# Final norm fused into one VectorE operation and the last two steps of the down product joined, in a one-core streaming-encoder block

## The chip, the cores and the metric

The kernel runs on one core of one Trainium2 chip. Its metric is the device time of one execution in microseconds (us); given is the median of three runs. The engines are TensorE (PE in the profile; PEld are its weight loads), VectorE (DVE), ScalarE (ACT), GpSimd (POOL) and SyncE (SP), which issues all the DMAs spoken of here.

## The reference

One trunk layer on x of 2048 tokens by 1024 features, in float32: a norm and an input projection, two mixer groups (a gated recurrence and stick-breaking attention), an output projection, then a SwiGLU feed-forward part and the final norm. Only its last lines matter here:

```python
h2 = rms_norm(x, norm_ffn[l])
gu = jnp.einsum('bsd,df->bsf', h2, w_ffn_in[l])
x = x + jnp.einsum('bsf,fd->bsd', jax.nn.silu(gu[..., :D_FF]) * gu[..., D_FF:], w_ffn_out[l])
return rms_norm(x, norm_final)      # x * rsqrt(mean(x * x) + 1e-6) * norm_final
```

## The kernel before, in words

The change lies in the last part, the product with `w_ffn_out` (2816 x 1024), called Down here, and the final norm. Down multiplies by Strassen's scheme: seven products (`DOWN`), each of one 512-wide combination of weight columns with a combination of activations. Its inner dimension comes in six steps (`NCH`): five of two blocks of 128 rows and a last one of one block. "Step (6,3)" is step 3 of product 6, the last product; the names of the profile leave the numbers out, so `blo` of step (6,3) is written `blo6_3` here.

- `operands` (L1116) loads a step's weights (`dr`, two loads and a sum on VectorE, L1135) and activations (`act`) and splits each into a rounded part, a cast on ScalarE (`bhi`, `a0hi`, `a1hi`, L1140), and the remainder, a subtraction (L1141): `blo` on VectorE, `a0lo` and `a1lo` on GpSimd. It is called two steps ahead (`LEAD`); each part has three buffers, so a cast for step c waits until TensorE has finished step c-3.
- `down_step` (L855) runs TensorE over two halves of 1024 tokens, and in a half over four row tiles of 128: per tile and block three matmuls (`mm3`, L149 to L151: `bhi` with `ahi`, `blo` with `ahi`, `bhi` with `alo`). A step of two blocks is 48 matmuls, the last one 24. A product's sums stay in eight banks of PSUM (`pw`); in its last step `use` (L1189) is called after each tile, and `add` (L1145) adds the tile to the residual `x2` (names `x`) on VectorE.
- A half has eight row tiles of output, 0 to 3 lower and 4 to 7 upper, each with two column halves, 0 and 1. Product 6 adds only to column half 0 of the lower tiles; all else is final once product 5 has ended.
- `finish` (L1154) squares and sums a tile's column half on ScalarE (`sqo`) and multiplies it by the final norm's weight on GpSimd (`o<-x,gfin`, L1164). `write` (L1166) computes the root for some tiles on VectorE: a sum (`ssp`, L1169) and 13 more tiny operations (`rsqrt_mean`, L124 to L137, names `ro_`). It then scales each `o` by the root: column half 0 on VectorE (L1181), 1 on ScalarE (L1179); one tile alone is done in a fused operation (L1176). It stores `o` from SP (L1182).

TensorE's instructions run in the order in which they are written. On the other engines a scheduler orders the instructions when the program is built, by its own estimate of when each is ready; each engine and SP then keep that order. `o` has twelve buffers (`OB`).

Of the kernel before, what the change touches and what calls it, by code (L numbers as in the profile page):

```python
# [9 lines left out]
F32 = mybir.dt.float32  # L10
# [3 lines left out]
ALU = mybir.AluOpType  # L14
# [3 lines left out]
P = 128  # L18
# [9 lines left out]
GT = 512  # L28
HT = 1024
NG = S // GT  # L30
TPG = GT // P
NHALF = S // HT
TPH = HT // P
# [34 lines left out]
DOWN = (  # L68
# [7 lines left out]
)  # L76
# [14 lines left out]
def tile_block(ctx: ExitStack, tc: tile.TileContext, x, w_in, w_out, w_gu, w_dn,  # L91
               g_mix, g_ffn, g_y, g_fin, lru_p, w_gate, out):
    nc = tc.nc
# [21 lines left out]
    NCH = -(-NPAIR // CH)  # L115
# [315 lines left out]
    for g in range(NG):  # L431
        starts.append(len(items))
        for h in range(H):
            for jj in range(TPG // 2):
                p = None
# [283 lines left out]
    end = []  # L719
# [132 lines left out]
    ps_u = banks.enter_context(tc.tile_pool(name="ps_u", bufs=2, space=PSUM, side="left"))  # L852
    pss = {}

    def down_step(p, c, bs, aa, use=None):  # L855

        m = len(bs)
        for half in range(NHALF):
            for t in range(TPG):
                if c == 0:  # L860
                    pss[half, t] = ps_u.tile([P, GT], F32, tag="abcd"[t], name=f"pw{half}_{p}_{t}")
                ts = slice(t * P, (t + 1) * P)
                for i, ((bhi, blo), (ahi, alo)) in enumerate(zip(bs, aa[half])):
                    mm3(pss[half, t], ahi[:, ts], alo[:, ts], bhi, blo,
                        c == 0 and i == 0, c == NCH - 1 and i == m - 1)
                if c == NCH - 1:
                    use(half, t, pss[half, t])


# [228 lines left out]
    with tc.manual_schedule(engines={mybir.EngineType.PE}), ExitStack() as dctx:  # L1098
        bp = dctx.enter_context(tc.tile_pool(name="bp", bufs=3, side="right"))
        x2p = dctx.enter_context(tc.tile_pool(name="x2p", bufs=1, side="left"))  # L1100
        op = dctx.enter_context(tc.tile_pool(name="op", bufs=OB, side="left"))
        gfin = x2p.tile([P, D], F32, name="gfin")

        x2s = {}

        def rows(half):
            if half not in x2s:
                x2s[half] = []
                for t in range(TPH):
                    xt = x2p.tile([P, D], F32, tag=f"x2_{half}_{t}", name=f"x2_{half}_{t}")  # L1110
                    gt = half * TPH + t
                    nc.sync.dma_start(out=xt, in_=x2_d[gt // TPG][gt % TPG * P:(gt % TPG + 1) * P, :])
                    x2s[half].append(xt)
            return x2s[half]

        def operands(p, c):  # L1116

            m = min(CH, NPAIR - c * CH)
            nm = f"{p}_{c}"
            ta = DOWN[p][0]  # L1120
            bb = []
            for j, k, _ in ta:
                t = bp.tile([P, m, GT], F32, tag="raw", name=f"dr{nm}_{j}{k}", bufs=4)
                r0 = c * CH * 2 * P
                src = w_dn[r0:r0 + 2 * m * P, k * GT:(k + 1) * GT].rearrange("(m j p) c -> j p m c", j=2, p=P)
                nc.sync.dma_start(out=t, in_=src[j])
                bb.append(t)
            aa = []
            for half in range(NHALF):
                sa = bp.tile([P, m, GT], F32, tag="act", name=f"act{half}_{nm}", bufs=4)  # L1130
                nc.sync.dma_start(out=sa, in_=act_d[half][p][c])
                aa.append(sa)
            sb = bb[0]
            if len(ta) == 2:
                nc.vector.tensor_tensor(out=sb, in0=bb[0], in1=bb[1], op=ALU.add if ta[1][2] > 0 else ALU.subtract)  # L1135
            out = []
            for q, src, eng in (("b", sb, nc.vector), ("a0", aa[0], nc.gpsimd), ("a1", aa[1], nc.gpsimd)):
                hi = bp.tile([P, m, GT], F32R, tag=f"{q}hi", name=f"{q}hi{nm}")
                lo = bp.tile([P, m, GT], F32R, tag=f"{q}lo", name=f"{q}lo{nm}")
                nc.scalar.copy(hi, src)  # L1140
                eng.tensor_tensor(out=lo, in0=src, in1=f32(hi), op=ALU.subtract)  # L1141
                out.append([(hi[:, i], lo[:, i]) for i in range(m)])
            return out

        def add(half, p, t, ps):  # L1145
            x2 = rows(half)
            for i, k, sign in DOWN[p][1]:
                xs = x2[i * TPG + t][:, k * GT:(k + 1) * GT]
                if sign > 0:
                    nc.vector.tensor_tensor(out=xs, in0=ps, in1=xs, op=ALU.add)  # L1150
                else:
                    nc.vector.tensor_tensor(out=xs, in0=xs, in1=ps, op=ALU.subtract)

        def finish(half, t0, n, ss, os, parts):  # L1154

            x2 = rows(half)
            for t in range(t0, t0 + n):
                for c in parts:
                    cs = slice(c * GT, (c + 1) * GT)
                    sq = op.tile([P, GT], F32, tag="sq", name=f"sqo{half}_{t}_{c}", bufs=1)  # L1160
                    nc.scalar.activation(sq, x2[t][:, cs], AF.Square, accum_out=ss[:, t, c:c + 1])  # L1161
                    o = os[t, c] = op.tile([P, GT], F32, tag="o", name=f"o{half}_{t}_{c}")
                    if (half, t, c) != (NHALF - 1, TPG - 1, 0):
                        nc.gpsimd.tensor_tensor(out=o, in0=x2[t][:, cs], in1=gfin[:, cs], op=ALU.mult)  # L1164

        def write(half, t0, n, ss, os):  # L1166
            x2 = rows(half)
            s2 = smp.tile([P, n], F32, tag=f"ssp{n}", name=f"ssp{half}_{t0}")
            nc.vector.tensor_tensor(out=s2, in0=ss[:, t0:t0 + n, 0], in1=ss[:, t0:t0 + n, 1], op=ALU.add)  # L1169
            rs = rsqrt_mean(s2, n, D, f"ro{half}_{t0}")  # L1170
            for t in range(t0, t0 + n):
                for c in range(2):
                    cs = slice(c * GT, (c + 1) * GT)
                    r = rs[:, t - t0:t - t0 + 1]
                    if (half, t, c) == (NHALF - 1, TPG - 1, 0):
                        nc.vector.scalar_tensor_tensor(out=os[t, c], in0=x2[t][:, cs], scalar=r, in1=gfin[:, cs],  # L1176
                                                       op0=ALU.mult, op1=ALU.mult)
                    elif c == 1:
                        nc.scalar.activation(os[t, c], os[t, c], AF.Copy, scale=r)  # L1179
                    else:  # L1180
                        nc.vector.tensor_scalar(out=os[t, c], in0=os[t, c], scalar1=r, scalar2=None, op0=ALU.mult)  # L1181
                    nc.sync.dma_start(out=out[half * HT + t * P:half * HT + (t + 1) * P, cs], in_=os[t, c])  # L1182

        work = [(p, c) for p in range(len(DOWN)) for c in range(NCH)]
        ready = [operands(*w) for w in work[1:1 + LEAD]]
        ss = [smp.tile([P, TPH, 2], F32, tag=f"sso{half}", name=f"sso{half}", bufs=1) for half in range(NHALF)]
        os = [{} for _ in range(NHALF)]

        def use(half, t, ps):  # L1189
            add(half, p, t, ps)  # L1190
            if p == len(DOWN) - 1:
                finish(half, t, 1, ss[half], os[half], (0,))
                if half == 0 and t == TPG - 1:
                    write(half, 0, TPG, ss[half], os[half])
                elif half and t >= TPG - 2:
                    write(half, *((0, TPG - 1) if t == TPG - 2 else (t, 1)), ss[half], os[half])

        for n, (p, c) in enumerate(work[1:]):
            bs, *aa = ready.pop(0)
            if n + 1 + LEAD < len(work):  # L1200
                ready.append(operands(*work[n + 1 + LEAD]))
            if n < NHALF:
                rows(n)
            if n == NHALF:
                nc.sync.dma_start(out=gfin, in_=g_fin.broadcast_to([P, D]))
            down_step(p, c, bs, aa, use)

            if p == len(DOWN) - 1 and c < NHALF:
                for t in range(TPG, TPH):
                    finish(c, t, 1, ss[c], os[c], (0, 1))  # L1210
                    if t % 2:
                        write(c, t - 1, 2, ss[c], os[c])
            if p == len(DOWN) - 1 and NHALF <= c < 2 * NHALF:
                finish(c - NHALF, 0, TPG, ss[c - NHALF], os[c - NHALF], (1,))
    banks.close()


# [51 lines left out]
```

## Time and profile before

| | us |
|---|---|
| median of 3 runs (2645.66 to 2648.19) | 2646.09 |
| profiled execution, its own time | 2647.3 |
| its span in the trace | 2645.6 |
| TensorE busy, 12680 matmuls | 2430.8 |
| VectorE busy | 1842.4 |
| ScalarE busy | 1262.6 |
| GpSimd busy | 1204.0 |

The span is the time from the first to the last instruction in the trace; times below are in us from its start. Busy time is summed over instructions; as they overlap at their ends, a busy engine need not be at its peak. In the view by time a row's two numbers are its start and how long it took, from its dispatch on, so that time in which an operation stood blocked is in it. An arrow in square brackets says how long the engine had been idle before the row and what ended that. The granted clock is a share of full speed: 1.00 is 2.4 GHz, 0.50 is 1.2 GHz.

### The profile page before, as it was taken

What the parts mean: (1) busy time and instruction counts of PE and PEld (TensorE: products, weight loads), DVE (VectorE), ACT (ScalarE), POOL (GpSimd) and SP (SyncE); (2) the same over time, 40 slices, a digit from 0 to 9 for tenths busy, and PEclk for the clock granted to TensorE, in tenths of its full rate; (3) what the DMA queues carried; (4) which work ended last, traced back from release to release, by engine and by line L of the source; (5) the groups of instructions that cost most, each with busy time, mean ns of one, the idle gap of its engine ahead of it and who ended that gap; (6) DMA issues with size and microseconds to landing.
All of it is one profiled execution on the core that took longest, in us unless ns stands there. A gap on an engine that the chain in (4) does not pass through costs nothing. (4 is left out here: it accounts for less than half of the span.)

```text
span 2645.6 us, 36918 instructions
## 1 busy us (share of the span) xinstructions
PE 2430.8 (92%) x12680; PEld 2046.7 (77%) x12680; DVE 1842.4 (70%) x2575; ACT 1262.6 (48%) x2285; POOL 1204.0 (46%) x1420
## 2 busy tenths in 40 slices
PE   7999999999888797897899979989999999999995
PEld 5888788787767697886777758868888887888884
DVE  4566888999999998997655545686655651644465
ACT  5556667576766575664333323343333322322233
POOL 5846433223244121122656654555545544744464
PEclk9999999999999898998999989999999999999997
DMA  7787886664556465654334443353232318745652
GB/s 249 266 288 250 269 267 211 209 210 143 176 179 208 152 223 169 206 188 151 123 121 137 157 167 100 108 177 114 100 103 97 111 69 323 257 153 183 196 172 104
DMA packets 221804, 468.57 MB, mean 177 GB/s; under 512 B 22704, under 2 KB 63664, under 8 KB 221616
## 3 DMA queue, kind: packets, MB, share of 16 engines
q1 hardware_dynamic: 221616, 466.21, 52.8%
q8 instruction: 100, 1.64, 0.3%
q14 instruction: 88, 0.72, 0.1%
HBM read 333.74 MB, written 132.38 MB: 176 GB/s over the span
## 5 line engine op out<-in xcount | busy, mean ns | idle before, releaser
L360 POOL MEMSET u<- 128x1 f32 x320 | 30.9, 98 | 559.2 <-DVE u L372 394.6
L372 DVE TENSOR_TENSOR_SCAN u<-u,u,zero 128x513 f32<-128x513 f32 x192 | 256.2, 1336 | 8.5 <-ACT u L362 8.0
L393 PE MATMUL t<-ident,be 128*128 128x128 f32 x1088 | 179.3, 281 | 59.0 <-DVE al L395 50.0
L378 DVE TENSOR_TENSOR be<-be,u 128x512 f32<-128x512 f32 (+2 forms) x320 | 215.4, 676 | 17.0 <-POOL be L366 1.4
L362 ACT ACTIVATE u<-z 128x512 f32<-128x512 f32 (+2 forms) x320 | 172.4, 539 | 99.1 <-PE z L358 65.2
L149 PE MATMUL pj<-ht_hi,w_hi 128*128 128x512 f32 x512 | 215.8, 421 | 2.3 <-DVE sl L291 1.5
L394 ACT CAST ah<-t 128x512 fp32r<-128x512 f32 (+2 forms) x320 | 168.7, 527 | 86.2 <-PE t L393 82.1
L393 PEld LDWEIGHTS t<-ident,be 128*128 128x128 f32 x1088 | 130.7, 143 | 98.5 <-DVE al L395 64.5
L151 PE MATMUL pj<-ht_hi,w_lo 128*128 128x512 f32 x512 | 202.8, 396 | 0.0
L150 PE MATMUL pj<-ht_lo,w_hi 128*128 128x512 f32 x512 | 201.9, 394 | 0.0
L358 PE MATMUL z<-ks,qd 128*128 128x512 f32 (+2 forms) x640 | 190.9, 380 | 7.1 <-ACT be L363 5.0
L395 DVE TENSOR_TENSOR al<-t,ah 128x512 fp32r<-128x512 f32 (+2 forms) x320 | 191.4, 599 | 7.5 <-ACT ah L394 7.1
L1088 POOL TENSOR_TENSOR e<-c,c 128x512 f32<-128x512 f32 x110 | 158.6, 1449 | 52.0 <-DVE c L1079 37.5
L363 ACT ACTIVATE be<-z 128x512 f32<-128x512 f32 (+2 forms) x320 | 172.5, 539 | 0.2
L408 PE MATMUL y<-ah,vs 128*128 128x256 f32 x576 | 149.9, 290 | 12.3 <-DVE yp L418 12.2
L149 PE MATMUL po<-wo_hi,yhi 128*128 128x256 f32 x512 | 154.9, 303 | 0.0
L372 DVE TENSOR_TENSOR_SCAN u<-u,zero 128x129 f32<-128x129 f32 (+3 forms) x128 | 112.3, 878 | 56.6 <-POOL u L366 55.0
L1141 DVE TENSOR_TENSOR blo<-dr,bhi 128x1024 fp32r<-128x1024 f32 (+1 forms) x41 | 81.8, 1995 | 98.5 <-ACT bhi L1140 98.5
L408 PE MATMUL y<-al,vs 128*128 128x256 f32 x576 | 147.8, 287 | 0.0
L151 PE MATMUL po<-wo_hi,ylo 128*128 128x256 f32 x512 | 145.7, 285 | 0.0
L150 PE MATMUL po<-wo_lo,yhi 128*128 128x256 f32 x512 | 145.6, 284 | 0.0
L1141 POOL TENSOR_TENSOR a0lo<-act,a0hi 128x1024 fp32r<-128x1024 f32 (+1 forms) x41 | 97.8, 2385 | 103.2 <-ACT a0hi L1140 103.2
(284 smaller groups left out, 7624.7 us busy)
## 6 DMA issues: line engine op xcount, KB each, us to landing
r<-in_w_gu SPq DMA_DIRECT2D x88, 512.0 KB, 3.9
act<-act_d SPq DMA_DIRECT2D x68, 512.0 KB, 4.2
dr<-in_w_dn SPq DMA_DIRECT2D x59, 512.0 KB, 4.5
act_d<-e SPq DMA_DIRECT2D x110, 256.0 KB, 2.0
w_hi<-w_d SPq DMA_DIRECT2D x50, 512.0 KB, 4.7
w_lo<-w_d SPq DMA_DIRECT2D x50, 512.0 KB, 5.5
vs<-vs_d SPq DMA_DIRECT2D x80, 256.0 KB, 3.6
ks<-ks_d SPq DMA_DIRECT2D x80, 256.0 KB, 3.6
```

Of the source, the lines that this page charges most:

```text
L149: nc.tensor.matmul(ps, lhsT=w_hi, rhs=m_hi, start=first, stop=False, skip_group_check=more)
L150: nc.tensor.matmul(ps, lhsT=w_hi, rhs=m_lo, start=False, stop=False, skip_group_check=more)
L151: nc.tensor.matmul(ps, lhsT=w_lo, rhs=m_hi, start=False, stop=last, skip_group_check=more)
L358: nc.tensor.matmul(z[:, :nz], lhsT=qd[:, i, qs], rhs=kss[p.c][:, :nz], start=i == 0, stop=i == 1)
L362: nc.scalar.activation(u[:, :n], z[:, :n], AF.Sigmoid, scale=-SCALE)
L363: nc.scalar.activation(be[:, :n], z[:, :n], AF.Sigmoid, scale=SCALE)
L372: nc.vector.tensor_tensor_scan(out=ur, data0=ur, data1=zero.broadcast_to([P, n + 1]), initial=1.0 if p.prev is None else p.prev.u[s][:, 0: ...
L378: nc.vector.tensor_tensor(out=p.be[s][:, :n], in0=p.be[s][:, :n], in1=p.u[s][:, 1:n + 1], op=ALU.mult)
L393: nc.tensor.transpose(tp[:, b, :], p.be[s][:, b * P:(b + 1) * P], ident)
L395: nc.vector.tensor_tensor(out=alo[:, :nb, s, :], in0=tp[:, :nb, :], in1=f32(ahi[:, :nb, s, :]), op=ALU.subtract)
L408: nc.tensor.matmul(y, lhsT=vs[:, b, :], rhs=t[:, b].rearrange("p s q -> p (s q)"), start=first and m == 0, stop=last and m == 1)
L1141: eng.tensor_tensor(out=lo, in0=src, in1=f32(hi), op=ALU.subtract)
```

## The change

Four things. The multiplication by `gfin` and the scaling by the root become one operation on VectorE (`x * r * gfin`) for all column halves but those of column half 1 of the lower tiles, which stay as they were. The upper tiles of a half get one root for four tiles instead of two roots for two, and they and the lower column halves 1 are now treated half by half over the steps (6,0) to (6,3). Half 1's lower tiles get roots for two, one and one tile instead of three and one. And steps (6,4) and (6,5) are run together: for each row tile nine matmuls in a row, then its `use`.

```diff
-    def down_step(p, c, bs, aa, use=None):
+    def down_step(p, c, bs, aa, use=None, end=None):
+        end = c == NCH - 1 if end is None else end
...
-                        c == 0 and i == 0, c == NCH - 1 and i == m - 1)
-                if c == NCH - 1:
+                        c == 0 and i == 0, end and i == m - 1)
+                if end:
                     use(half, t, pss[half, t])
...
-                    o = os[t, c] = op.tile([P, GT], F32, tag="o", name=f"o{half}_{t}_{c}")
-                    if (half, t, c) != (NHALF - 1, TPG - 1, 0):
+                    if t < TPG and c:
+                        o = os[t, c] = op.tile([P, GT], F32, tag="o", name=f"o{half}_{t}_{c}")
                         nc.gpsimd.tensor_tensor(out=o, in0=x2[t][:, cs], in1=gfin[:, cs], op=ALU.mult)
...
-                    if (half, t, c) == (NHALF - 1, TPG - 1, 0):
+                    if (t, c) not in os:
+                        os[t, c] = op.tile([P, GT], F32, tag="o", name=f"o{half}_{t}_{c}")
                         nc.vector.scalar_tensor_tensor(out=os[t, c], in0=x2[t][:, cs], scalar=r, in1=gfin[:, cs],
                                                        op0=ALU.mult, op1=ALU.mult)
-                    elif c == 1:
+                    else:
                         nc.scalar.activation(os[t, c], os[t, c], AF.Copy, scale=r)
-                    else:
-                        nc.vector.tensor_scalar(out=os[t, c], in0=os[t, c], scalar1=r, scalar2=None, op0=ALU.mult)
...
-                elif half and t >= TPG - 2:
-                    write(half, *((0, TPG - 1) if t == TPG - 2 else (t, 1)), ss[half], os[half])
+                elif half and t:
+                    write(half, *((0, 2) if t == 1 else (t, 1)), ss[half], os[half])
...
+            if n == len(work) - 3:
+                held = bs, aa
+                continue
+            if n == len(work) - 2:
+                bs, aa = held[0] + bs, [x + y for x, y in zip(held[1], aa)]
             down_step(p, c, bs, aa, use)
 
-            if p == len(DOWN) - 1 and c < NHALF:
-                for t in range(TPG, TPH):
-                    finish(c, t, 1, ss[c], os[c], (0, 1))
-                    if t % 2:
-                        write(c, t - 1, 2, ss[c], os[c])
-            if p == len(DOWN) - 1 and NHALF <= c < 2 * NHALF:
-                finish(c - NHALF, 0, TPG, ss[c - NHALF], os[c - NHALF], (1,))
+            if p == len(DOWN) - 1 and c < 2 * NHALF:
+                half, late = c // 2, c % 2
+                finish(half, TPG + 2 * late, 2, ss[half], os[half], (0, 1))
+                if late:
+                    write(half, TPG, TPG, ss[half], os[half])
+                    finish(half, 0, TPG, ss[half], os[half], (1,))
```

How the instructions stand on the engines shows three places. In these rows `o0_4_1` is half 0, tile 4, column half 1, `ssp1_4` the sum of half 1 that begins with tile 4, and the last number of a name tells buffers apart.

On VectorE, the operations ahead of `blo6_3`, before (the tiny ones of each root but the first and last left out):

```order
L1169 TENSOR_TENSOR ssp0_4_25527<-sso0_23027 128x2
...
L1181 TENSOR_SCALAR o0_4_0_25513<-o0_4_0_25513,ro0_4_y2_25552 128x512
L1181 TENSOR_SCALAR o0_5_0_25521<-o0_5_0_25521,ro0_4_y2_25552 128x512
...
L1181 TENSOR_SCALAR o0_6_0_25564<-o0_6_0_25564,ro0_6_y2_25603 128x512
L1181 TENSOR_SCALAR o0_7_0_25572<-o0_7_0_25572,ro0_6_y2_25603 128x512
L1169 TENSOR_TENSOR ssp1_4_25698<-sso1_23028 128x2
...
L1181 TENSOR_SCALAR o1_4_0_25684<-o1_4_0_25684,ro1_4_y2_25723 128x512
L1181 TENSOR_SCALAR o1_5_0_25692<-o1_5_0_25692,ro1_4_y2_25723 128x512
L1141 TENSOR_TENSOR blo6_3_25623<-dr6_3_10_25613,bhi6_3_25622 128x1024
```

and now:

```order
L1142 TENSOR_TENSOR blo6_2_25444<-dr6_2_10_25434,bhi6_2_25443 128x1024
L1170 TENSOR_TENSOR ssp0_4_25596<-sso0_23027 128x4
...
L1178 SCALAR_TENSOR_TENSOR o0_4_0_25623<-x2_0_4_23055,ro0_4_y2_25621,gfin_22990 128x512
...
L1178 SCALAR_TENSOR_TENSOR o0_7_1_25644<-x2_0_7_23061,ro0_4_y2_25621,gfin_22990 128x512
L1136 TENSOR_TENSOR dr6_5_10_25740<-dr6_5_10_25740,dr6_5_11_25742 128x512
L1142 TENSOR_TENSOR blo6_3_25529<-dr6_3_10_25519,bhi6_3_25528 128x1024
```

One root of 14 tiny operations and eight fused ones now stand ahead of `blo6_3`, where three roots and six scalings stood. The other root and the other eight fused operations of the upper tiles stand between `blo6_3` and `blo6_4`.

On GpSimd, the instructions around the subtractions for step (6,4), before:

```order
L1141 TENSOR_TENSOR a1lo6_3_25631<-act1_6_3_25619,a1hi6_3_25630 128x1024
L1164 TENSOR_TENSOR o0_0_1_25855<-x2_0_0_23047,gfin_22990 128x512
...
L1164 TENSOR_TENSOR o1_2_1_25948<-x2_1_2_23133,gfin_22990 128x512
L1141 TENSOR_TENSOR a0lo6_4_25798<-act0_6_4_25788,a0hi6_4_25797 128x1024
L1164 TENSOR_TENSOR o1_3_1_25952<-x2_1_3_23135,gfin_22990 128x512
L1141 TENSOR_TENSOR a1lo6_4_25802<-act1_6_4_25790,a1hi6_4_25801 128x1024
L1141 TENSOR_TENSOR a0lo6_5_25883<-act0_6_5_25873,a0hi6_5_25882 128x512
```

and now, with what each waits for (DMAHW is a lane of DMAs, here a store or a load that must have landed):

```order
L1142 TENSOR_TENSOR a1lo6_3_25537<-act1_6_3_25525,a1hi6_3_25536 128x1024 [waits DMAHW3_49,PE_49,Activation_49]
L1142 TENSOR_TENSOR a0lo6_4_25677<-act0_6_4_25667,a0hi6_4_25676 128x1024 [waits DMAHW5_49,PE_49,Activation_49]
L1165 TENSOR_TENSOR o1_0_1_25870<-x2_1_0_23129,gfin_22990 128x512 [waits DMAHW3_49,DMAHW1_49,DVE_49]
L1165 TENSOR_TENSOR o1_1_1_25874<-x2_1_1_23131,gfin_22990 128x512 [waits DMAHW4_49,DMAHW2_49,DVE_49]
L1142 TENSOR_TENSOR a1lo6_4_25681<-act1_6_4_25669,a1hi6_4_25680 128x1024 [waits DMAHW6_49,PE_49,Activation_49]
L1165 TENSOR_TENSOR o1_2_1_25878<-x2_1_2_23133,gfin_22990 128x512 [waits DMAHW5_49,DVE_49]
L1165 TENSOR_TENSOR o1_3_1_25882<-x2_1_3_23135,gfin_22990 128x512 [waits DMAHW6_49,DVE_49]
L1142 TENSOR_TENSOR a0lo6_5_25754<-act0_6_5_25744,a0hi6_5_25753 128x512 [waits DMAHW1_49,PE_49,Activation_49]
```

The four multiplications of half 1 now stand behind `a0lo6_4`, two of them ahead of `a1lo6_4` and all ahead of `a0lo6_5`; `o1_0_1` takes the buffer of half 1's `o1_4_0`, so it waits for a store of half 1's upper tiles.

On TensorE, the first row tile of the end, before (rows that read alike left out):

```order
L149 MATMUL pw0_6_0_25455<-bhi6_4_25793,a0hi6_4_25797 128x512
...
L151 MATMUL pw0_6_0_25455<-bhi6_4_25793,a0lo6_4_25798 128x512
...
L151 MATMUL pw1_6_3_25504<-bhi6_4_25793,a1lo6_4_25802 128x512
L149 MATMUL pw0_6_0_25455<-bhi6_5_25878,a0hi6_5_25882 128x512
L150 MATMUL pw0_6_0_25455<-blo6_5_25879,a0hi6_5_25882 128x512
L151 MATMUL pw0_6_0_25455<-bhi6_5_25878,a0lo6_5_25883 128x512
```

and the first row tile now:

```order
L149 MATMUL pw0_6_0_25455<-bhi6_4_25672,a0hi6_4_25676 128x512
...
L151 MATMUL pw0_6_0_25455<-bhi6_4_25672,a0lo6_4_25677 128x512
L149 MATMUL pw0_6_0_25455<-bhi6_5_25749,a0hi6_5_25753 128x512
L150 MATMUL pw0_6_0_25455<-blo6_5_25750,a0hi6_5_25753 128x512
L151 MATMUL pw0_6_0_25455<-bhi6_5_25749,a0lo6_5_25754 128x512
L149 MATMUL pw0_6_1_25462<-bhi6_4_25672,a0hi6_4_25676 128x512
```

The three matmuls with step (6,5)'s operands follow six of step (6,4) in the same row tile, where they followed all 48.

## Rows read from the trace of the kernel before

**Rows 1.** The page's first line.
```profile
span 2645.6 us, 36918 instructions
```

**Rows 2.** Windows: length, each engine's busy time (instructions), granted clock, DMA share, GB/s.
```profile
2590.00:2600.00 10.00, 9.55 (x30) 7.70 (x31) 8.16 (x15) 4.04 (x11) 7.33 (x5) 0.69 0.42 147
...
2605.00:2610.00 5.00, 2.34 (x5) 1.68 (x6) 3.39 (x2) 4.10 (x10) 3.77 (x3) 0.64 0.00 2
```

**Rows 3.** Waits from 2480 us: who for whom, total us, times, longest.
```profile
PE pw L150 <- DVE blo L1141: 10.9, 2, 8.8
...
PE pw L149 <- ACT bhi L1140: 1.5, 1, 1.5
```

**Rows 4.** TensorE by time: start, duration, engine, line, operation, [idle before <-released by].
```profile
2570.38 0.39 PE L149 MATMUL pw<-bhi,a0hi 128*128 128x512 f32 x1
...
2581.26 0.39 PE L149 MATMUL pw<-bhi,a0hi 128*128 128x512 f32 x1
...
2590.45 0.80 PE L150 MATMUL pw<-blo,a0hi 128*128 128x512 f32 x1 [8.80 <-DVE blo L1141]
...
2603.65 0.39 PE L151 MATMUL pw<-bhi,a1lo 128*128 128x512 f32 x1
...
2605.54 0.50 PE L149 MATMUL pw<-bhi,a0hi 128*128 128x512 f32 x1 [1.50 <-ACT bhi L1140]
...
2608.16 0.79 PE L150 MATMUL pw<-blo,a0hi 128*128 128x512 f32 x1 [2.12 <-DVE blo L1141]
...
2621.77 0.39 PE L151 MATMUL pw<-bhi,a0lo 128*128 128x512 f32 x1
...
2626.53 0.39 PE L151 MATMUL pw<-bhi,a1lo 128*128 128x512 f32 x1
```

**Rows 5.** VectorE by time, same columns.
```profile
2552.32 1.53 DVE L1135 TENSOR_TENSOR dr<-dr,dr 128x1024 f32<-128x1024 f32 x1 [0.80 <-DMA dr<-in_w_dn]
...
2580.26 2.29 DVE L133 TENSOR_TENSOR ro_a<-ro_y 128x2 f32<-128x2 f32 x1
...
2582.58 1.18 DVE L135 TENSOR_TENSOR ro_b<-ro_a,ro_v 128x2 f32<-128x2 f32 x1
...
2589.18 1.22 DVE L1141 TENSOR_TENSOR blo<-dr,bhi 128x1024 fp32r<-128x1024 f32 x1
...
2598.53 0.16 DVE L135 TENSOR_TENSOR ro_b<-ro_a,ro_v 128x2 f32<-128x2 f32 x1
...
2598.72 0.16 DVE L137 SCALAR_TENSOR_TENSOR ro_y<-ro_b,ro_y 128x2 f32<-128x2 f32 x1
...
2600.15 0.88 DVE L1181 TENSOR_SCALAR o<-o,ro_y 128x512 f32<-128x512 f32 x2
```

**Rows 6.** GpSimd by time.
```profile
2580.16 2.37 POOL L1141 TENSOR_TENSOR a1lo<-act,a1hi 128x1024 fp32r<-128x1024 f32 x1
...
2582.49 4.92 POOL L1164 TENSOR_TENSOR o<-x,gfin 128x512 f32<-128x512 f32 x4
```

**Rows 7.** ScalarE by time.
```profile
2600.14 1.34 ACT L1179 ACTIVATE o<-o,ro_y 128x512 f32<-128x512 f32 x2 [6.00 <-issue]
...
2604.45 1.04 ACT L1140 CAST bhi<-dr 128x1024 fp32r<-128x1024 f32 x1
```

**Rows 8.** The end by time, VectorE and ScalarE.
```profile
2622.20 4.09 DVE L1150 TENSOR_TENSOR x<-pw,x 128x512 f32<-128x512 f32 x6 [12.11 <-PE pw L151]
...
2622.98 0.63 ACT L1161 ACTIVATE sqo<-x 128x512 f32<-128x512 f32 x1 [13.81 <-DVE x L1150]
...
2623.52 0.19 ACT L1161 ACTIVATION_READ_ACCUMULATOR sqo<-x 128x1 f32 x1
...
2638.32 0.74 DVE L1176 SCALAR_TENSOR_TENSOR o<-x,ro_y,gfin 128x512 f32<-128x512 f32 x1
```

**Rows 9.** SP's last store; stores from 2630 us: count, size, median us to landing.
```profile
2641.50 0.59 SPq L1182 DMA_DIRECT2D out<-o  x1
...
out<-o SPq DMA_DIRECT2D x16, 256.0 KB, 2.8
```

## The prediction

> **What bounds it now.** I read the page first, then the waits of TensorE in the last 100 us, then one engine after another in order of time. The span is 2645.6 us [rows 1]; everything the diff touches lies after 2541 us, so only this stretch counts. The reader is to see that TensorE loses its granted clock there: mean 0.69 and 0.64 in two windows [rows 2]. It stops for `blo`, 10.9 us in two waits, and for `bhi`, 1.5 us [rows 3]. In time [rows 4]: step (6,2) begins at 2570.38 and (6,3) at 2581.26, so 48 matmuls take 10.88 us, 0.2267 each. The second matmul of (6,3) comes at 2590.45 instead of 2581.49; step (6,4) begins at 2605.54, 1.89 after the matmul before it, and its second matmul waits until 2608.16. From the start of (6,3) to the last matmul, 2626.53, are 119 intervals: 26.98 us at full clock, 45.27 in fact. **18.3 us** are lost: 13.0 in the three late starts (8.96, 1.66, 2.39), 5.3 in matmuls after them at the 1.2 GHz level, before the clock is back at 2.4.
>
> Why are the operands late? `blo6_3` takes only 1.22 us, but starts at 2589.18, and VectorE had no idle time before it [rows 5]: it was busy with other work. Ahead of it on VectorE stand three roots of 14 tiny operations. Such an operation, given a quiet GpSimd, follows the one before at 0.195 us (2598.53 to 2598.72) [rows 5]. But the one at 2582.58 takes 1.18 and the one at 2580.26 takes 2.29 [rows 5], while GpSimd does four multiplications in 4.92 us and, from 2580.16, a 2.37 us subtraction [rows 6]: VectorE gets one in per GpSimd instruction. `bhi6_4` is late in turn: ScalarE stood 6.00 us before a scaling that needs the same slow root, and the cast comes only at 2604.45 [rows 7].
>
> **The change, part by part.** GpSimd loses 23 of 31 multiplications by `gfin`, some 23 x 1.23 = 28 us. ScalarE loses 8 of 16 scalings, those ahead of the casts. VectorE has six roots instead of seven (84 tiny operations, not 98), and 24 fused operations (0.74 us, the only row of its kind, without GpSimd beside it [rows 8]) instead of 15 scalings (two in 0.88 [rows 5]) and one fused: 24 x 0.74 - 15 x 0.44 - 0.74 = 10.4 us more. That extra is hidden only while VectorE has its `blo` ready before TensorE asks, so I walk through it.
>
> *To `blo6_3`.* VectorE starts with the sum `dr6_4`, released by its load at 2552.32 [rows 5]. Then: that sum and `blo6_2`, 2 x 1.22; 14 tiny, 2.73; eight fused, 5.92; sum `dr6_5`, 0.68 (the adds of [rows 8], 4.09 for six); `blo6_3`, 1.22: 13.0 us. GpSimd has three subtractions (2.37) and four multiplications (1.23): 12.0. If none of it overlaps, `blo6_3` ends at 2577.3; TensorE asks at 2581.49. GpSimd idles at the start, since its cast `a0hi6_3` now stands behind two more squares on ScalarE; I credit 2 us of overlap for that and take 2575.4. So the first stall goes, with 4 to 6 us to spare.
>
> *To the joined step.* It starts at 2581.26 + 10.88 = 2592.14 and asks for `blo6_4` at 2592.37, `blo6_5` at 2593.73 and `a0lo6_5` at 2593.95; before, the last two were asked for 48 matmuls, 10.9 us, later. The change adds a wait here: GpSimd's multiplication `o1_0_1` reuses the buffer of `o1_4_0`, so it waits until that has been written out, and `a1lo6_4`, `a0lo6_5` and `a1lo6_5` queue behind it. The second root ends at 2575.4 + 2.73 = 2578.1, the first fused at 2578.9, its write lands 2.8 later [rows 9]: 2581.7, when five fused operations are done. From there I alternate, one by one: 1.23, fused 0.74, 1.23, fused, `a1lo6_4` 2.37, fused, 1.23, `blo6_4` 1.22 (2591.2), 1.23, `blo6_5` 0.68 (2593.1), `a0lo6_5`, taken as another 1.23 (2594.4). The first two are in time by 0.6 to 1.2 us, the last is 0.5 late. I charge **0.5 us** and no loss of clock, which shows only after the stops of 8.96 and of 1.66 with 2.39 [rows 4]. The bounds of the uncovered price: fused operations at the 0.68 of a two-input add and more overlap give 0; no overlap at all is rival 1. The casts `bhi6_4` and `a0hi6_4` have no scaling ahead of them any more and wait only for buffers, free at 2570; all are early. On SP the two loads `act6_5` move ahead of four stores, behind the eight of half 0: issued near 2574, they feed `a0lo6_5` and `a1lo6_5`, which start after 2593. Covered.
>
> *The tail.* Before, 19.07 us lie between the last matmul and the end. Now the last matmul is at 2581.26 + 26.98 + 0.5 = 2608.7. Tile 3 of half 0 is done 36 matmuls into the joined step, its last one at 2600.6, its add 0.43 later (as 2622.20 follows 2621.77 [rows 4, 8]), the square 0.78 after that, its sum 0.73 later still [rows 8]: 2602.5. Root and two adds, 2.73 + 2 x 0.68: 2606.6. Four fused, 2.96: 2609.6. The add of the last tile starts behind them and one more add at 2610.4, its sum of squares is ready at 2611.9, and then come about 15 interleaved tiny operations (1.2), two fused, three tiny, one fused, nine tiny in a chain (1.75), the last fused: 6.4 us, so 2618.3, and the last store at 2618.8. Before, the last store was issued at 2641.50, 4.1 before the end, behind others; alone, it cannot be shorter than about a landing, 2.8 [rows 9]. Of these bounds I take the middle, 3.4: **2622.2**. The tail shrinks from 19.07 to 13.5 us, by 5.6.
>
> **Sum.** 18.3 - 0.5 + 5.6 = 23.4 us off the span of 2645.6, so 2622.2. The profiled execution took 2647.3, 1.7 more than its span, and would take 2623.9; it lies 1.2 above the median of the runs, 2646.09. Forecast for the median: **2622.7 us**, 0.9% less.
>
> The rule that speaks against it: the Trainium skill, "SBUF — State Buffer", section "Who interferes with whom", says that VectorE instructions with two SBUF inputs and GpSimd's reads of SBUF share one read interface, and that whoever comes second stands fully blocked. The rows of the tiny operations agree (1.18 us for 0.16 of work). By it a fused operation, with two inputs from SBUF, is as exposed as what it replaces; rival 1 is what that makes of the time here.
>
> **Rivals.**
> 1. *The exchange stays one for one where it matters.* For: eight fused operations stand directly ahead of `blo6_4`, and six GpSimd instructions fall beside them. With no overlap from 2577.3: VectorE 2.73 + 5.92 + 1.22 + 0.68, GpSimd 5 x 1.23 + 2.37, 19.1 in all: `a0lo6_5` at 2596.4, 2.5 late. Like the stop of 1.66 and 2.39, that may halve the clock, 2.6 us (half of the 5.3). Against the forecast 2.0 + 2.6 more: **2627**. Against: GpSimd stands still until 2581.7.
> 2. *The tiny operations are slow of themselves*, not through GpSimd. Then 14 take 17.1 us: `blo6_3` at 2579.6, still in time, but `blo6_4` at 2579.6 + 17.1 + 5.9 + 1.2 = 2603.8, 11.4 late, with 2.6 of clock. 18.3 - 14.0 + 5.6 = 9.9 off: **2636**. Against: the same operations at 0.195 in a later root.
> 3. *Slower.* TensorE stops inside the joined step for `a0lo6_5`, because GpSimd waits for a store. It decides if the first store of half 1 lands late: every us after 2581.1 costs one. To lose the 23.4 and 5.3 more it must land near 2610, as it would if VectorE's queue before it were delayed by 28 us; GpSimd has 12 us of work there. That gives **2652**. Only an order on the queues that I misread allows it.
> 4. *The change doesn't do what it says*: TensorE is given back its time, but half clock or the stores' rate (eight stores on the queue) sets the end: 2640 to 2646.
>
> **Numbers.** Forecast (2618 to 2625) 0.70; rival 1 0.15; rival 2 0.05; rival 4 0.07, of which 0.05 within the bound below; rival 3 0.03. A measurement here can tell about 0.2%, 5.3 us, from no change. The range runs from no stall and fused operations at the 0.68 of an add (eight on the tail's path, 0.5 us less, and 0.5 of stall), with 3.5 us for the rough parts of the tail, 2618, to rival 1 with 3 us more, 2630. Faster 0.92, same 0.05, slower 0.03.
>
> **What would show it.** Right: tiny operations near 0.2 us from 2571 on; no wait of `pw` for `blo` over 1 us; granted clock 1.00 until the last matmul, near 2608.7; the last fused operation near 2618. Rival 1: a wait for `blo6_4` or `a0lo6_5` of 2 us and a dip of the clock after 2592. Rival 2: tiny operations of 1.2 us beside an idle GpSimd. Rival 3: a wait for `a0lo`, GpSimd idle for a store beyond 2585. The prediction is wrong if step (6,3) still waits, or if the tail takes over 16 us.

## The result and the profile after

| | before | after |
|---|---|---|
| median of 4 runs each, us | 2645.93 | **2611.67** (2608.38 to 2616.12) |
| ratio, 95% interval | | 0.987 (0.9851 to 0.9888) |
| profiled execution's own time | 2647.3 | 2616.12 |
| start of step (6,3) | 2581.26 [rows 4] | 2574.84 |
| start of the last matmul | 2626.53 [rows 4] | 2601.81 |
| span | 2645.6 [rows 1] | 2614.4 |

Faster by 1.3%, 34.3 us between the medians. The forecast was 2622.7, the range 2618 to 2630: the time lies below it. The profiled execution happens to be the slowest of the four, so the spans differ by less, 31.2 us.

The page of after, its first line:

```profile
span 2614.4 us, 36856 instructions
```

TensorE by time (start, duration; no row from 2500 us on shows idle time before it), and two windows over this stretch, to compare with [rows 2]:

```profile
2574.84 0.39 PE L149 MATMUL pw<-bhi,a0hi 128*128 128x512 f32 x1
...
2585.72 0.39 PE L149 MATMUL pw<-bhi,a0hi 128*128 128x512 f32 x1
...
2601.81 0.39 PE L151 MATMUL pw<-bhi,a1lo 128*128 128x512 f32 x1
```

```profile
2570.00:2606.00 36.00, 32.20 (x143) 26.32 (x141) 27.19 (x74) 10.38 (x24) 12.92 (x7) 1.00 0.35 129
2590.00:2600.00 10.00, 10.00 (x46) 8.26 (x44) 6.08 (x21) 3.70 (x11) 0.00 (x0) 1.00 0.01 2
```

From the start of (6,3) to that of the last matmul are 26.97 us, where before took 45.27: the three late starts and the half clock, 18.3 us, are gone to the last tenth, and the granted clock stays at 1.00. VectorE by time shows why:

```profile
2549.15 2.31 DVE L133 TENSOR_TENSOR ro_a<-ro_y 128x4 f32<-128x4 f32 x1
2551.50 1.22 DVE L135 TENSOR_TENSOR ro_b<-ro_a,ro_v 128x4 f32<-128x4 f32 x1
...
2559.48 7.54 DVE L1178 SCALAR_TENSOR_TENSOR o<-x,ro_y,gfin 128x512 f32<-128x512 f32 x8
...
2567.54 1.21 DVE L1142 TENSOR_TENSOR blo<-dr,bhi 128x1024 fp32r<-128x1024 f32 x1
...
2570.65 0.16 DVE L133 TENSOR_TENSOR ro_a<-ro_y 128x4 f32<-128x4 f32 x1
2570.85 0.16 DVE L135 TENSOR_TENSOR ro_b<-ro_a,ro_v 128x4 f32<-128x4 f32 x1
...
2571.24 9.60 DVE L1178 SCALAR_TENSOR_TENSOR o<-x,ro_y,gfin 128x512 f32<-128x512 f32 x8
2580.77 4.00 DVE L1142 TENSOR_TENSOR blo<-dr,bhi 128x1024 fp32r<-128x1024 f32 x2
...
2609.77 0.75 DVE L1178 SCALAR_TENSOR_TENSOR o<-x,ro_y,gfin 128x512 f32<-128x512 f32 x1
```

and GpSimd beside it:

```profile
2549.03 2.42 POOL L1142 TENSOR_TENSOR a0lo<-act,a0hi 128x1024 fp32r<-128x1024 f32 x1 [2.97 <-ACT a0hi L1141]
2551.40 5.08 POOL L1165 TENSOR_TENSOR o<-x,gfin 128x512 f32<-128x512 f32 x4
...
2574.24 3.25 POOL L1165 TENSOR_TENSOR o<-x,gfin 128x512 f32<-128x512 f32 x2 [11.09 <-DMA out<-o]
...
2584.18 1.74 POOL L1142 TENSOR_TENSOR a0lo<-act,a0hi 128x512 fp32r<-128x512 f32 x1
```

While GpSimd works (2549 to 2559) VectorE gets one tiny operation in per GpSimd instruction, 1.22 or 2.31 us, as in [rows 5]. While GpSimd stands 11.09 us for the store of `o1_4_0`, the second root runs at 0.2 us an operation. When GpSimd is back, the eight fused operations take 9.60; the first eight, with one subtraction of GpSimd beside them, took 7.54.

So this stretch gave 24.8 us: from the start of (6,3) to the end are 39.56 us, before 64.34. But (6,3) itself starts 6.42 us earlier, in code that the change does not touch, and that part the prediction did not have. TensorE's matmuls ahead of it stand in the same order in both programs. What differs is where the tiles lie. The small buffers of the roots are allocated early, one set for each number of tiles; the changed kernel has no root for three tiles any more, that set is gone, and all that is allocated behind it on the left of SBUF lies 416 bytes lower. TensorE's operands in the up stage (the product with `w_ffn_in`, 44 rounds of seven products of twelve matmuls, 1250 to 2172 us in the changed kernel), by the built programs, in bytes in a partition:

| | before | after |
|---|---|---|
| weights of products 0 and 6 | 67456 | 67040 |
| tokens of product 0 (as those of products 1 to 4, on the right) | 135136 | 135136 |
| tokens of product 6 (on the left) | 36736 | 36320 |
| tokens less weights modulo 256: product 0, product 6 | 96, 0 | 0, 0 |

In all rounds, products 0 to 4 are 96 bytes apart before and 0 now: 2640 of the stage's 3696 matmuls.

### The profile page after: what moved, and what is told of

The parts are those of the page before. It is cut to its first block, busy times and chain, and to the rows that moved or that the text cites. A ratio compares the mean times of both kernels' runs of the same rounds, so it can differ in the third digit from the quotient of the medians.

```text
span 2614.4 us, 36856 instructions
## 1 busy us (share of the span) xinstructions
PE 2417.2 (92%) x12680; PEld 2046.0 (78%) x12680; DVE 1837.1 (70%) x2569; ACT 1258.0 (48%) x2277; POOL 1174.2 (45%) x1397
## 4 chain that ended last, share of the span: by engine, by line
PE 43%; DVE 3%; DMA 2%; POOL 2%; issue 2%; ACT 1%; SPq 0%; POOLq 0%; DVEq 0%; ACTq 0%
PE pw L151 5%; PE pw L150 5%; PE pw L149 5%; PE psc L149 3%; PE psa L149 3%; PE psc L150 3%; PE psc L151 3%; PE psa L150 3%; PE psa L151 3%; PE psd L149 3%; PE psd L150 3%; PE psd L151 3%; PE psb L149 1%; PE psb L150 1%; PE psb L151 1%
## 5 line engine op out<-in xcount | busy, mean ns | idle before, releaser
L360 POOL MEMSET u<- 128x1 f32 x320 | 31.2, 99 | 558.0 <-DVE u L372 393.4
```

## The experiments

Times are medians, and ratios with their 95% interval are to the kernel before on the same chip (2647.94 for experiments 1, 2, 6 and 7, 2647.83 for 4 and 5, 2647.00 for 8, 2646.68 for 9). The changed kernel's 2611.67 stands beside a before of 2645.93; where a run on another chip is set against it, the difference by the two ratios is given too.

**1. The change at the old addresses.**

```diff
     smp = ctx.enter_context(tc.tile_pool(name="smp", bufs=2))
+    ctx.enter_context(tc.tile_pool(name="padp", bufs=1)).tile([P, 104], F32, name="pad")
```

> The changed kernel with one unused tile of 416 bytes behind the small pool, so that the large tiles lie again at the SBUF addresses that they had before the change (the program is otherwise the same). Theory A (the time won ahead of product 6 comes from the addresses, which the change moved by 416 bytes when the roots for three tiles went): between 1780 and 2200 us about 1780 matmuls, as before, not 1802; product 5's last adds about 6.4 us later than in the changed kernel; time 2611.7 + 6.4 = 2618, up to 2622. Theory B (chance, the traces differ from execution to execution): about 1802 matmuls and 2608 to 2616. Both: the end from product 5's adds on unchanged, no wait of TensorE.

Measured 2622.15 us (0.9902; 0.9887 to 0.9917), 10.5 more than the changed kernel, 8.5 by the ratios. Step (6,3) starts at 2583.00, 8.2 later. In its trace the two products' pace differs. The first matmuls of product 6 (`psb<-b`), of the next product 0 (`psa<-b`) and of product 1 (`psc<-t`):

```profile
1301.94 0.39 PE L150 MATMUL psb<-b,a1h 128*128 128x512 f32 x1
...
1304.66 0.40 PE L150 MATMUL psa<-b,a1h 128*128 128x512 f32 x1
...
1307.47 0.39 PE L150 MATMUL psc<-t,s3h 128*128 128x512 f32 x1
```

and the same three in the changed kernel:

```profile
1301.07 0.39 PE L149 MATMUL psb<-b,a1h 128*128 128x512 f32 x1
...
1303.79 0.39 PE L149 MATMUL psa<-b,a1h 128*128 128x512 f32 x1
...
1306.51 0.39 PE L149 MATMUL psc<-t,s3h 128*128 128x512 f32 x1
```

Twelve matmuls of product 6 take 2.72 us in both, 227 ns each. Those of product 0 take 2.81 at the old addresses, 234 each, and 2.72 at the new. Nothing waits there; each matmul is a little longer. Windows from 1780 to 2200 us (TensorE's count second), the old addresses and the changed kernel:

```profile
1780.00:2200.00 420.00, 414.54 (x1782) 334.74 (x1781) 240.33 (x269) 134.55 (x208) 214.07 (x139) 0.99 0.31 106
```

```profile
1780.00:2200.00 420.00, 413.42 (x1802) 338.22 (x1801) 246.55 (x268) 138.27 (x211) 220.77 (x141) 0.99 0.32 111
```

Theory A holds, with a time at the upper end of what it gave. The end of this run is the changed kernel's: last matmul 12.62 us before the end, no wait.

**2. The kernel before at the new addresses.**

```diff
+        w = 4 if n == 3 else n
-        v = smp.tile([P, n], F32, tag=f"v{n}", name=f"{name}_v")
+        v = smp.tile([P, w], F32, tag=f"v{w}", name=f"{name}_v")[:, :n]
...
```

and the same for the root's other buffers.

> The kernel before with the root for three tiles in the buffers of the root for four: the large tiles lie 416 bytes lower, as in the changed kernel, and nothing else changes but the order of some tiny operations in the last 20 us. Theory A: about 1802 matmuls between 1780 and 2200 us, time 2645.9 - 6.4 = 2639.5, down to 2635. Theory B: about 1780 matmuls and 2645.9 within 2. Both: the three late starts of steps (6,3) and (6,4), 13 us, stay.

2638.78 us (0.9968; 0.9956 to 0.9979), 9.2 less than before, with 1802 matmuls in the same window and step (6,3) started at 2574.64. The stalls stay: 8.80, 1.59 and 2.13 us. So 416 bytes without any other change are worth 9.2 us, and the change at unchanged addresses (experiment 1 against before) 25.8.

**3. The distance by itself.** Matmuls alone, for 26 pairs of offsets:

```python
for n, (wo, mo) in enumerate(combos):
    ...
    ms = [t[:, mo // 4:mo // 4 + GT] for t in m]
    for k in range(triples):
        ws = [t[:, wo // 4 + k % 3 * P:wo // 4 + k % 3 * P + P] for t in w]
        ...
```

> No part of the reference: 48 matmuls (mm3 sixteen times) for each of 26 pairs of offsets of the weights' and of the moving tile's address, from bases that are multiples of 2048 bytes; once with the other engines idle and once beside VectorE, ScalarE and GpSimd at work and stores. Theory A1 (what counts is the distance of the two addresses, as the changed kernel has them equal modulo 512 bytes and the kernel before 96 apart): 227 ns with equal offsets (and 512 and 1024 apart), 231 ns or more at 96 and most others, whichever of the two is moved. A2 (the weights' address alone counts): slow where the weights are at 384 and fast at 480, whatever the other. A3 (the place in SBUF decides only against other engines' accesses): 227 ns for all in the idle pass, differences in the busy one. Theory B (no dependence): 227 ns throughout.

One tile each; the two numbers at the end are the first and the last start of its 16 matmuls of line 121, which are 45 intervals apart. Offsets (weights, tokens) 0 and 0, 0 and 96, 0 and 256, 384 and 480 (the kernel before), 480 and 480 (after), and 0 and 96 beside the other engines:

```profile
L121 PE MATMUL qa<-mhi,whi x16: 389/389/389, 50.3 to 60.5; 128*128 128x512 f32 x16
...
L121 PE MATMUL qd<-mhi,whi x16: 394/394/403, 83.4 to 93.9; 128*128 128x512 f32 x16
...
L121 PE MATMUL qi<-mhi,whi x16: 389/389/395, 139.4 to 149.6; 128*128 128x512 f32 x16
...
L121 PE MATMUL qx<-mhi,whi x16: 396/399/399, 305.6 to 316.1; 128*128 128x512 f32 x16
...
L121 PE MATMUL qy<-mhi,whi x16: 387/389/396, 316.8 to 327.1; 128*128 128x512 f32 x16
...
L121 PE MATMUL bd<-mhi,whi x16: 394/394/402, 392.2 to 402.7; 128*128 128x512 f32 x16
```

10.2 us over 45 is 227 ns, 10.5 is 233. All eight pairs whose distance is a multiple of 256 bytes (0, 256, 512, 1024, -256, and equal offsets) are at 227 to 228 ns, two (64 and 320) at 229, all others at 232 to 234. What counts is the tokens' offset less the weights', modulo 256, not the place: 384 and 480 run as 0 and 96, and weights moved by 64 (233 ns) as tokens moved by 192. The pass beside busy engines differs from the idle one by less than 1 ns. A1 holds, with 256 in the place of 512; A2, A3 and B fall. The Trainium skill ("TensorE: Matmul & The Clock Gate", section "Step-by-step: what each phase is for") says that weights and the moving operand come through two independent read ports, so that loading weights takes nothing from a running matmul. By that rule, if nothing else counted, all pairs would run at one pace; measured are 227 and 233 ns, so the measurement decides.

**Which weights, the matmul's own or the next one's?** Matmuls alone again, two kinds alternating:

```python
for k in range(2 * pairs):
    wo, mo = two[k % 2]
    ...
    nc.tensor.matmul(ps, lhsT=w[k % 2][:, c:c + P], rhs=m[k % 2][:, mo // 4:mo // 4 + GT],
                     start=k == 0, stop=k == 2 * pairs - 1)
```

> No part of the reference: 48 matmuls for each of ten patterns in which two matmuls alternate, with offsets of weights and moving tile for the first and for the second; d is 96, 128 and 32 bytes. Pattern 1, control: all offsets 0. Pattern 2: (0, 0) and (d, d), so that each matmul agrees with its own weights and is d away from the next one's. Pattern 3: (0, d) and (d, 0), each d away from its own weights and in agreement with the next one's. Pattern 4: (0, d) throughout. Theory N (the next matmul's weights are loaded while this one's tile streams, and these two get in each other's way): pattern 2 at 229 ns or more, pattern 3 at 227, pattern 4 at 232 to 234. Theory O (a matmul's own two operands count): pattern 2 at 227, patterns 3 and 4 at 232 to 234. If only what lies at the same address in both counts otherwise, patterns 2 and 3 fall between.

The control and the three patterns for d = 96, the first of the two rows of each (46 intervals from its first to its last start):

```profile
L121 PE MATMUL qa<-mhi,whi x24: 389/389/389, 50.9 to 61.4; 128*128 128x512 f32 x24
...
L121 PE MATMUL qb<-mhi,whi x24: 391/394/400, 61.8 to 72.6; 128*128 128x512 f32 x24
...
L121 PE MATMUL qc<-mhi,whi x24: 392/397/397, 73.1 to 83.6; 128*128 128x512 f32 x24
...
L121 PE MATMUL qd<-mhi,whi x24: 392/394/399, 84.1 to 94.8; 128*128 128x512 f32 x24
```

Mean from start to start, in ns, by the view by time, which has hundredths of a microsecond:

| d | pattern 2 | pattern 3 | pattern 4 |
|---|---|---|---|
| 96 | 233.9 | 230.0 | 233.6 |
| 128 | 228.4 | 229.9 | 232.1 |
| 32 | 231.8 | 230.5 | 233.3 |

The control is at 226.7. N and O both fall as put: the full pace came only where a moving tile agrees with both weights, its own and the next one's. Why stays open.

**4. Two more distances in the kernel**: the unused tile of experiment 1 with 256 and with 128 bytes.

> The changed kernel with an unused tile of 256 bytes: the large tiles on the left lie 256 bytes higher, still a multiple of 256 bytes from those on the right. If the distance modulo 256 bytes is what counts: 227 ns in the up stage, 1802 matmuls between 1780 and 2200 us, 2608 to 2616 as the changed kernel. If any shift from the changed kernel's addresses costs: 1780 and about 2622.

> The changed kernel with an unused tile of 128 bytes, so that products 0 to 4 of the up stage take their weights and their tokens 128 bytes apart modulo 256. If the distance modulo 256 counts: 233 ns there, as in the measurement of offsets, 1780 matmuls or fewer between 1780 and 2200 us, 2620 to 2626. If only 512 or 2048 or the first addresses matter: another figure, 2612 or between.

2614.01 us (0.9869; 0.9854 to 0.9884) and 2620.57 us (0.9899; 0.9884 to 0.9914). 256 bytes cost nothing that can be told: the window from 1780 to 2200 us has 1793 matmuls and not the 1802 expected, but those with nothing between them follow at 227 ns as in the changed kernel. 128 cost 6.6 us against 256 on the same chip, and 1783 matmuls fit into the window. So the distance modulo 256 counts in the kernel too.

**5. Everything aligned, meant to beat both.**

```diff
+    const.tile([P, 24], F32, name="pad0")
     ident = const.tile([P, P], F32, name="ident")
...
-        u = p.u[s] = atp.tile([P, GT + 1], F32, tag="u", name=f"u{p.nm}_{s}", bufs=UB)
+        u = p.u[s] = atp.tile([P, GT + 64], F32, tag="u", name=f"u{p.nm}_{s}", bufs=UB)
```

and the same for `xpad`, with 160 bytes behind the small pool.

> A version meant to beat both: the changed kernel with every tile that TensorE reads at the same address modulo 256 bytes (attention's and the recurrence's tiles, 32 to 160 bytes off in both kernels, and the identity matrix). If those distances cost there too, some of the 6900 matmuls ahead of the up stage lose 4 to 7 ns each now: 5 to 20 us less than the changed kernel, 2592 to 2607. If those stages are bound elsewhere, or their matmuls already stand in pairs that agree: 2608 to 2614.

2612.77 us (0.9867; 0.9851 to 0.9884): no gain. The theory that the first 1200 us lose in the same way fell. The matmuls of 512 columns in the input projection (`pj`) agree modulo 256 in all three kernels and still follow each other at 230 ns on average in each (starts less than 0.26 us apart), so something else holds them; what it is stays open. Those of 256 columns that weigh the values in attention (`y`) are 128 bytes apart in the changed kernel and aligned here, and take 124 ns in both. So the cost of the distance is shown for 512 columns only.

**6. The joined steps alone**: the kernel before with the lines of the diff on `end` and `held`.

> The kernel before with steps (6,4) and (6,5) run together, and nothing else of the change; addresses as before. If the parts add up as predicted: the wait of 8.8 us for blo6_3 and those of about 1.5 and 2.1 at the joined step stay, the tail shrinks by 5.6 us, and step (6,5)'s remainders, asked for 10.9 us earlier and made from 2608 on, cost up to 1.5 us: 2640 to 2642. Rival (the joined step alone gives most of the gain, since the late starts are made up at the end): below 2632.

```profile
2590.57 0.79 PE L150 MATMUL pw<-blo,a0hi 128*128 128x512 f32 x1 [9.01 <-DVE blo L1142]
...
2605.64 0.49 PE L149 MATMUL pw<-bhi,a0hi 128*128 128x512 f32 x1 [1.63 <-ACT bhi L1141]
...
2608.26 0.50 PE L150 MATMUL pw<-blo,a0hi 128*128 128x512 f32 x1 [2.13 <-DVE blo L1142]
...
2626.14 0.39 PE L151 MATMUL pw<-bhi,a1lo 128*128 128x512 f32 x1
```

2642.85 us (0.9979; 0.997 to 0.9989), 5.1 less, where 2640 to 2642 was expected; the rival falls. All three waits stay, and the last matmul is 14.76 us before the end of the span of 2640.9, where before had 19.07: 4.3 off the tail instead of 5.6.

**7. All but the joined steps**: the changed kernel without the five lines on `held`.

> The changed kernel with steps (6,4) and (6,5) one after the other again: fused operations, one root for four tiles and the new addresses stay. If the parts add up: no late start of TensorE and clock 1.00 to the last matmul, but a tail near the 19.07 us of before instead of 12.5: 2611.7 + 5.6 to 6.5 = 2617 to 2618. Rival as for the joined step alone: above 2630.

2619.73 us (0.9895; 0.9881 to 0.9908), 19.05 less than the kernel before at the same, new, addresses (2638.78). No wait of TensorE; the last matmul starts at 2601.17 of 2619.1, so the tail is 17.9 us. The time is 1.7 us above the 2618 expected. The parts: 19.05 for the stalls with 1.1 of tail, and for joining on top 8.06 between the medians, 6.6 by the ratios and 5.3 in the tails of the two traces (17.9 and 12.6).

**8. Fusion undone, one root kept.**

```diff
-                    if t < TPG and c:
+                    if t >= TPG or c:
```

and in `write` the scalings of before for these.

> The changed kernel with the upper tiles' multiplication by gfin on GpSimd again and their scaling on VectorE and ScalarE; one root for four tiles, the joined steps and the new addresses stay. Prediction's theory (GpSimd's multiplications beside the tiny operations made blo6_3 late): GpSimd has 16 more of 1.23 us, up to 22 us of work beside some 9 us of VectorE's ahead of blo6_3, so tiny operations of 1.2 to 2.3 us all along both roots and a late start of step (6,3) or of the joined step of 2 to 9 us, with half clock behind the larger of these: 2614 to 2630. Rival (the one root for four in place of two, and the new order, did it): no wait of TensorE, 2611 to 2613.

2628.44 us (0.9928; 0.9914 to 0.9942), 16.8 more than the changed kernel, 15.3 by the ratios. Step (6,3) starts on time, but the joined step does not:

```profile
2588.86 0.49 PE L149 MATMUL pw<-bhi,a0hi 128*128 128x512 f32 x1 [2.55 <-ACT bhi L1141]
2590.13 0.76 PE L150 MATMUL pw<-blo,a0hi 128*128 128x512 f32 x1 [0.77 <-DVE blo L1142]
2593.21 0.80 PE L149 MATMUL pw<-bhi,a0hi 128*128 128x512 f32 x1 [0.62 <-ACT bhi L1141]
2594.44 0.79 PE L150 MATMUL pw<-blo,a0hi 128*128 128x512 f32 x1 [0.43 <-DVE blo L1142]
2599.23 0.79 PE L151 MATMUL pw<-bhi,a0lo 128*128 128x512 f32 x1 [3.99 <-POOL a0lo L1142]
```

8.4 us of waits, for three engines in turn, and the granted clock is at 0.62 between the two levels from 2588 to 2606: from the start of (6,3) to the last matmul are 40.51 us (2575.28 to 2615.79) instead of 26.97, 5.2 more than the waits. Of the two places that the prediction's theory named, the stop is at the second, and its size is within the 2 to 9 us; the rival falls.

**9. One root undone, fusion kept.**

```diff
-                    write(half, TPG, TPG, ss[half], os[half])
+                    write(half, TPG, 2, ss[half], os[half])
+                    write(half, TPG + 2, 2, ss[half], os[half])
```

> The changed kernel with two roots of two tiles again for each half's upper tiles; the operations stay fused, the steps joined, the addresses as in the changed kernel. Prediction's theory (a tiny operation costs 0.2 us once GpSimd has little to do): the 14 more of each half cost some 2.7 us of VectorE, blo6_3 is taken up near 2570 instead of 2567.5 and is asked for near 2575: no wait of TensorE, 2610 to 2615. Rival (the fewer roots removed the late start of (6,3), by however slow operations): 14 more at 1.2 us put blo6_3 7 us late: 2618 or more.

2619.15 us (0.9898; 0.9882 to 0.9915), 7.5 more than the changed kernel, and neither theory had it right. `blo6_3` is taken up at 2564.64, well in time; the stop is one step later, for `blo6_4`. TensorE, then VectorE:

```profile
2585.65 0.61 PE L150 MATMUL pw<-blo,a0hi 128*128 128x512 f32 x1 [3.54 <-DVE blo L1142]
```

```profile
2573.14 2.31 DVE L133 TENSOR_TENSOR ro_a<-ro_y 128x2 f32<-128x2 f32 x1
2575.49 1.21 DVE L135 TENSOR_TENSOR ro_b<-ro_a,ro_v 128x2 f32<-128x2 f32 x1
...
2581.72 2.74 DVE L1178 SCALAR_TENSOR_TENSOR o<-x,ro_y,gfin 128x512 f32<-128x512 f32 x4
2584.38 1.82 DVE L1142 TENSOR_TENSOR blo<-dr,bhi 128x1024 fp32r<-128x1024 f32 x2
```

The fourth root does not fit into GpSimd's wait for the store any more: GpSimd is back at 2571.80, and seven of its operations, 1.2 us or more each, stand one for one against GpSimd's instructions.

## Why the prediction was wrong by 11 us, and where it was right

**Wrong: "everything the diff touches lies after 2541 us, so only this stretch counts."** This first step failed, and it makes most of the miss. The matmuls ahead of 2541 us are the same, but the roots' buffers belong to a pool that is allocated near the start, so dropping the root for three tiles moved TensorE's operands of the up stage 416 bytes, from 96 bytes apart to a multiple of 256. That was worth some 9 us: 9.2 in experiment 2 against before, 10.5 between the medians of the changed kernel and experiment 1, 8.5 by their ratios. The rest of the 11 is the edited stretch, 25.8 instead of 23.4. With the addresses put back, experiment 1 has a span of 2622.6 and a median of 2622.15; forecast were 2622.2 and 2622.7. So close an agreement is partly luck: before ran 2 us longer on that chip, and the ratio 0.9902 gives 2620.0 on the first.

The stage gains less than the pace alone gives. In the traces of experiment 2 and of before, matmuls of the up stage with nothing between them (starts less than 0.26 us apart) follow at 227.1 instead of 232.0 ns, which is 18 us over the 3696. From the first start to the last the stage takes only 8.8 less, 919.75 instead of 928.50, since the time lost in longer intervals grew from 71.2 to 80.5. Most of that growth is in product 4, whose weight load waits for `u`, an addition of VectorE, more often now. Who waits for whom from 1254 to 2154 us (total, times, longest), before and in the changed kernel:

```profile
PEld psc L149 <- DVE u L954: 20.3, 8, 12.7
```

```profile
PEld psc L149 <- DVE u L955: 28.0, 22, 12.4
```

So a TensorE that runs faster there has given back half of it in waits for others.

**Right: the stalls, 18.3 us.** 45.27 became 26.97.

**Right in the time, open in the cause: why they go.** `blo6_3` was to be ready 6.1 us before TensorE asks (2575.4 against 2581.49); it ended at 2568.75, 6.3 before 2575.06. But this stop needed neither of the two remedies by itself: it is gone with one root and GpSimd's multiplications kept (experiment 8), and with two roots and fused operations (experiment 9). What these two share with the changed kernel is the new order, in which half 1's first root stands behind `blo6_3`. In the trace of before, that root's sum starts at 2575.21, and the cast `bhi6_3` on ScalarE ends at 2578.24; `blo6_2` had taken 2.32 us:

```profile
2553.77 2.32 DVE L1141 TENSOR_TENSOR blo<-dr,bhi 128x1024 fp32r<-128x1024 f32 x1
...
2575.21 1.25 DVE L1169 TENSOR_TENSOR ssp<-sso 128x2 f32<-128x2 f32 x1
```

```profile
2577.19 1.05 ACT L1140 CAST bhi<-dr 128x1024 fp32r<-128x1024 f32 x1
```

By an estimate from these rows, `blo6_3` ahead of that root would have ended near 2580.6, 0.9 us before it was asked for. So the order alone may cure this stop; no run has the order alone. It is the joined step that needs both remedies, 8.4 us of waits without the one and 3.5 without the other.

**Too careful: the 0.5 us stall at the joined step.** It was 0. `blo6_4` and `blo6_5` were both done at 2584.77 and `a0lo6_5` at 2585.92; they were asked for at 2585.94, 2587.31 and 2587.53 (its start, 2585.72, and one, seven and eight matmuls of 0.2267). GpSimd's wait for a store came as named and was free: its first multiplication starts 0.6 us before (6,3), where 0.4 after it was forecast, and from there to the end of `a0lo6_5` it needed 11.7 us, forecast 12.7. So rival 1, the one-for-one exchange that reaches TensorE, did not happen, though the exchange is there: eight fused operations in 9.60 us instead of 7.54.

**A little long: the tail, 13.5 us.** It takes 12.59 (2601.81 to 2614.4), 6.5 less than the 19.07 of before, where 5.6 was forecast. From the last matmul to the end of the last fused operation 8.7 us passed instead of 9.6 (2608.7 to 2618.3 in the forecast); from there to the end it was 3.9, as forecast. Joining gives 4.3 of this alone, the fused operations 1.1 alone, both together 6.5.

So the sum on the edited stretch, 23.4 us, measured 24.8 in the trace and 25.8 in the medians at unchanged addresses. The other rivals fell with the same rows: tiny operations beside an idle GpSimd take 0.16 us (rival 2), `a0lo6_5` came before it was asked for (rival 3), and TensorE's time reached the end (rival 4).

## What to carry to other kernels

An edit that adds or drops a small buffer moves everything that is allocated behind it, also in stages that it does not touch: compare the addresses of TensorE's two operands before and after, modulo 256 bytes, and in the trace first ask when the unedited code ahead of the edit ended. Tiny VectorE operations cost what GpSimd's neighbours cost, so count GpSimd's instructions beside them; taking those away, having fewer tiny operations, and moving them behind the operand that TensorE asks for next are separate remedies, and which of them a stop needs depends on where it stands.

## What was not expected of the hardware

- A float32r matmul of 128 x 128 with 512 columns follows the one before at 227 ns when the weights and the moving tile lie a multiple of 256 bytes apart in a partition, and at 229 to 234 ns at the other distances tried, with all other engines idle or busy alike (experiment 3). In the kernel that was 9.2 us of 2648 (experiment 2), and no wait shows it: only the starts do. It is not enough that a matmul agrees with its own weights; those of the next one count too. Nor does agreement always bring 227: the `pj` matmuls of experiment 5 agree and take 230.
- A single stop of TensorE of 3.54 us (experiment 9) is followed by eight matmuls some 0.43 us apart, at a granted clock of 0.50 (window below), the 1.2 GHz level; the prediction charged no clock for short stops.

```profile
2586.00:2589.00 3.00, 3.00 (x8) 2.31 (x7) 0.20 (x1) 0.00 (x0) 0.00 (x0) 0.50 0.03 11
```
